# Where the second half's last scores and the meta tokens' lists are kept and sent, in a two-layer conv/attention/expert trunk on one core

## The chip, the cores and the metric

The kernel runs on one core of one Trainium2 chip. The time is device microseconds of one execution; three runs of the kernel before lie between 1829.51 and 1835.26, with the median at 1833.64.

## What is computed

272 tokens (16 meta tokens in front of 256) of 1024 float32 numbers go through two layers. Each layer is a mixer (convolution and attention, gated) and a PEER stage, in which every token picks, for each of 8 heads, 16 of 16384 experts:

```python
def _peer(h, wq, keys, u_table, v_table):
    q = (hf @ wq).reshape(T, PEER_HEADS, 2, PEER_HALF)
    s = jnp.einsum('thpd,hpnd->thpn', q, keys)
    sv, si = lax.top_k(s, PEER_TOPK)
    cand = (sv[:, :, 0, :, None] + sv[:, :, 1, None, :]).reshape(T, PEER_HEADS, PEER_TOPK * PEER_TOPK)
    cidx = (si[:, :, 0, :, None] * N_KEYS + si[:, :, 1, None, :]).reshape(...)
    top_s, top_pos = lax.top_k(cand, PEER_TOPK)
    eidx = jnp.take_along_axis(cidx, top_pos, axis=-1)
    gw = jax.nn.softmax(top_s.astype(jnp.float32), axis=-1).astype(h.dtype)
...
    def block(args):
        xb, ib, wb = args
        a = jnp.einsum('ted,td->te', u_table[ib], xb)
        act = jax.nn.gelu(a) * wb
        return jnp.einsum('te,ted->td', act, v_table[ib])
```

The output is the 256 tokens behind the meta tokens.

## The kernel before

Everything is float32, with channels on partitions. The order on each engine is the order in which the program is written; loops hand control to generators (`early`, `routes`, `gathers`, `wbuild`) a step at a time, so that work of different parts is mixed by hand. A tile's memory comes from pools; an instruction that writes a new tile waits for the last readers of what lay there.

**The end of the mixer.** `scores(i, qT_)` runs for 16 key tiles `i` (8 heads, 2 lists each). TensorE puts the scores of the first 128 tokens (`k` = 0) and of the second 128 (`k` = 1) side by side into a PSUM tile `sc`, and in layer 0 those of the meta tokens into `scm`. `top16` on VectorE picks 16 values and their places for each row: five instructions a tile, into `sv`, `si` (and `svm`, `sim` for the meta tokens). For the last four tiles (`i` of 12 and up) ScalarE first copies both halves to a tile `cp` in the mixer's pool `mp`; the second half's rows are put on the list `behind`. They are taken up only after `heads(0, 0)` and `heads(0, 1)`, which turn the first half's lists into experts (`ef`) and weights, packed into `ew` (L920). Then the mixer's pools close (`mixs.close()`).

**The expert stage** opens pools where the mixer's memory was: `X`, and `ga` with `iww` (experts and weights spread by head), `xs`, `xr`, and four buffers `gb`. Two ways lead through it. The last 160 of the 272 tokens use all experts: TensorE multiplies `xh` with every tile of `u` (the matmuls of `A`, 128 steps, each 8 matmuls that stand as 16 instructions in the trace) and later the result with every tile of `v` (the matmuls of `po`). The other tokens, two groups of 64 and 32 and in layer 0 the 16 meta tokens, gather their experts: one indirect DMA on POOL's queue brings 128 rows of `u` and `v`, 1 MB (`gb`, L1105); VectorE multiplies (L1133) and adds up (L1115, L1117). The `u` and `v` tiles come through SP's queue, four tiles of 1 MB ahead (`wraw`).

**What stands at the seam, in order.** POOL: `spread(0)`, which sends `ew` to `iww`; four gathers; `spread(1)`; then, in layer 0, eight small transfers that put the meta tokens' lists `svm`, `sim` in the layout of the others (`mv`, `mi`, L1003); then a gather for each group of rows that VectorE has added. VectorE: the four rows of `behind`; the tiles `zs`; the packing of weights (L1013 to L1015); in layer 0 `second(mv, mi, ...)`, the meta tokens' experts; then the gathers' work, mixed with `heads(1, 0)` and `heads(1, 1)` for the second half. ScalarE: `xs` (L963); two tables `tx` of the meta tokens (L806); copies of `A` to `X`; `xr` (L972). TensorE: 9 steps of `A`; the transposes of `xs` (L971); 6 steps; the transposes of `ef` for the first half (L1026); 16 steps; transposes for the next group; 5 steps; the transposes for the second half. The transposes share two PSUM buffers `wp`, so those of L1026 need a buffer that `xr` has emptied.

`idxT` (128 x 3 x 256 half-precision) and `wlo` (128 x 256 float32) are tiles that stay for the whole kernel. They are written behind the transposes of L1026 (L1027, L1028) and read by `wbuild`.

Of the kernel before, what the change touches and what calls it, by code (L numbers as in the profile page):

```python
# [7 lines left out]
F32 = mybir.dt.float32  # L8
# [3 lines left out]
U32 = mybir.dt.uint32  # L12
AF = mybir.ActivationFunctionType
# [7 lines left out]
T = 272  # L21
# [22 lines left out]
def trunk_kernel(ctx: ExitStack, tc: tile.TileContext, a: dict, out: bass.AP, dbg=None, stop=None):  # L44
    nc = tc.nc
    V, S, G, PE = nc.vector, nc.scalar, nc.gpsimd, nc.tensor
# [4 lines left out]
    def mm(o, l, r, start, stop):  # L51
        PE.matmul(o, l, r, start=start, stop=stop, skip_group_check=True)  # L52
# [81 lines left out]
    idxT = pp.tile([128, 3, 256], F16, name="idxT")  # L134
    wlo = pp.tile([128, 256], F32, name="wlo")
# [5 lines left out]
    def run_all(g):  # L141
        for _ in g:
            pass
# [32 lines left out]
    for l in range(NL):  # L176
        last = l == NL - 1
# [7 lines left out]
        rpool = rp.enter_context(tc.tile_pool(name=f"route{l}", bufs=1, side="right"))  # L185
# [40 lines left out]
        else:  # L226

            p = zp.tile([128, 512], F32, name="z", bufs=3)
# [59 lines left out]
        def attention():  # L288
# [99 lines left out]
            pk = aps()  # L388
            for i, (q0, n) in enumerate(QT):
                PE.transpose(pk[0:8, q0:q0 + n], rr[:n, i * 16 + 8:i * 16 + 16], ident[:n, :n])  # L390
            rk = mp.tile([8, T], F32, name="rk")
            S.activation(rk, pk[0:8, :T], AF.Copy)
            yield
            yield
# [364 lines left out]
        def scores(i, qT_):  # L759
            p = sp.tile([128, 512], F32, name="sc", bufs=2)  # L760
            for k, (q0, n) in enumerate(QT[:2]):
                mm(p[:, k * 128:(k + 1) * 128], qT_[:, q0:q0 + n], keys[:, i], True, True)
            if not last:

                if i % 4 == 0:
                    ohp["m"] = sp.tile([128, 512], F32, name="scm")
                q = i % 4
                mm(ohp["m"][32 * q:32 * q + 32, 0:128], qT_[:, 0:32], keys[:, i], True, True)
            if i >= 12:
                p_, p = p, mp.tile([128, T], F32, name="cp", bufs=4)[:, 0:256]  # L770
                S.activation(p, p_[:, 0:256], AF.Copy)
                if not last and i == 15:
                    m_, ohp["m"] = ohp["m"], mp.tile([128, T], F32, name="sk", bufs=2)[:, 0:128]
                    S.activation(ohp["m"], m_[:, 0:128], AF.Copy)
            rows = []
            for k in range(2):
                w = mp.tile([128, 128], F32, name=f"tkw{k}")
                rows.append((sv[:, k, i], si[:, k, i], p[:, k * 128:(k + 1) * 128], w))
            if not last and i % 4 == 3:
                rows.append((svm[:, i // 4], sim[:, i // 4], ohp["m"][:, 0:128], mp.tile([128, 128], F32, name="tkw2")))  # L780
            if i >= 12:
                behind.append(rows.pop(1))
            top16(rows)
# [100 lines left out]
        for i in range(16):  # L884
            z = ztile(t0)
            qT_ = mp.tile([128, T], F32, name="qr", bufs=2)
            S.activation(qT_[:, t0:], z, AF.Copy)
            if i == 0:
                st = sp.tile([128, 512], F32, name="st")
                sums(st[:, :TQ], sq[:, :, t0:], 1)  # L890
            if pend is not None:
                scores(i - 1, pend)
            pend = qT_
            if i == 1:
                rs = rstd(st[:, :TQ], D, TQ, "m")
            if i == 4 and not last:
                rsm = mp.tile([128, 128], F32, name="rsm")
                V.tensor_copy(rsm.rearrange("p (t h) -> p t h", h=8), rs[:, 0:16, None].to_broadcast([128, 16, 8]))
            if i == 8:

                pr_ = sp.tile([128, 512], F32, name="st")
                rsT = rpool.tile([128, 3], F32, name="rsT")
                nr = 2 if last else 3
                for k, (q0, n) in enumerate(QT[:2]):
                    PE.transpose(pr_[:, k * 128:(k + 1) * 128], rs[:, q0 - t0:q0 - t0 + n], ident)
                if not last:
                    PE.transpose(pr_[:, 256:384], rsm, ident)
            if i == 9:
                V.tensor_copy(rsT[:, 0:nr], pr_[:, 0:nr * 128].rearrange("p (k x) -> p k x", x=128)[:, :, 0])
            if i >= 9:  # L910
                next(early, None)
            if 4 <= i < 12:
                c = i - 4
                G.tensor_tensor(xh[:, c, t0:], xg[:, c, t0:], rs, op=OP.mult)  # L914
        scores(15, pend)
        run_all(early)
        run_all(heads(0, 1))

# [72 lines left out]
        def routes():  # L991
            done["e"] = ohp["ew"]
            spread(0)
            done["g"] = 1
            yield
            if not last:

                mv = rpool.tile([128, 1, 2, 16], F32, name="mv")
                mi = rpool.tile([128, 1, 2, 16], U32, name="mi")
                for q in range(4):  # L1000
                    for d_, s_ in ((mv, svm), (mi, sim)):
                        d4 = d_.rearrange("(n x) o s b -> x n o s b", x=2)[q // 2, :, 0, q % 2]
                        G.dma_start(d4, s_[32 * q:32 * q + 16])  # L1003
            r2 = ohp["r"]
            for k in range(2):
                if k:
                    yield from heads(k, 0)
                    yield from heads(k, 1)
                ew, ef = ohp["ew"], ohp["ef"]
                ts = ew[:, :, 1]  # L1010

                wh_ = r2.tile([128, 128], F16, name="w16")
                V.tensor_scalar(h8(wh_), ts, WS, None, op0=OP.mult)  # L1013
                V.tensor_copy(ef[:, 2], wh_)
                V.scalar_tensor_tensor(h8(ef[:, 3]), ts, WS, h8(ef[:, 2]), op0=OP.mult, op1=OP.subtract)  # L1015
                if k == 0:
                    if not last:
                        yield
                        im = r2.tile([128, 2, 16], F32, name="im")
                        yield from second(mv, mi, 1, rsT[:, 2:3], im, iww[-1][:, :, 1])  # L1020
                        V.scalar_tensor_tensor(iww[-1].bitcast(I32)[:, 0, 0], im[:, 0], 128.0, im[:, 1], op0=OP.mult, op1=OP.add)
                for _ in range(LAG + (7 if last and k == 0 else 0)):
                    yield
                p = pW.tile([128, 512], F32, name="wp", bufs=2)
                for q in range(4):
                    PE.transpose(p[:, q * 128:(q + 1) * 128], ef[:, q], ident)  # L1026
                S.activation(idxT[:, :, k * 128:(k + 1) * 128], p[:, 0:384].rearrange("p (a b) -> p a b", a=3), AF.Copy)  # L1027
                S.activation(wlo[:, k * 128:(k + 1) * 128], p[:, 384:512], AF.Copy)  # L1028
                yield
# [308 lines left out]
```

## Time and profile before

| | before |
|---|---|
| median of 3 runs | 1833.64 us |
| profiled execution, its own time | 1828.79 us |
| its span | 1827.0 us |
| TensorE busy | 1764.6 us (97%) |
| VectorE busy | 1143.9 us (63%) |
| ScalarE busy | 421.6 us (23%) |
| POOL busy | 324.2 us (18%) |
| DMA | 559.37 MB, mean 306 GB/s |

TensorE is busy for nearly the whole span, so what counts are the places where it is not. The slices of the span show two where its share falls inside the kernel: one around 320 to 365 us, the end of layer 0's mixer, and a lesser one around 1235 to 1280 us, the end of layer 1's. The two matrix products of the expert stage follow them, and with them the DMA queues run full.

### The profile page before, as it was taken

To read this page: it belongs to the slowest core of one execution; us is meant where nothing else is said; L and a number is where in the kernel's file an instruction comes from. 1 tells how busy PE (TensorE), PEld (TensorE's weight loads), DVE (VectorE), ACT (ScalarE), POOL (GpSimd) and SP (SyncE) were. 2 spreads that over 40 slices of the span, in tenths; PEclk is the share of its full clock that TensorE was granted. 3 is DMA by queue.
4 is the path that set the end of the run, shared out by engine and by line. 5 is a ranking of instruction groups with operands and counts; after the bars stand their busy time and mean duration, and the time that the engine had idled before them with its cause. 6 is when DMAs were issued, how large, how long until landed. Compare 5 with 4: busy or idle time off the path is not lost.

```text
span 1827.0 us, 29396 instructions
## 1 busy us (share of the span) xinstructions
PE 1764.6 (97%) x11611; PEld 1629.9 (89%) x11611; DVE 1143.9 (63%) x3101; ACT 421.6 (23%) x1225; POOL 324.2 (18%) x393
## 2 busy tenths in 40 slices
PE   9999999599999999999999999998999999999998
PEld 7678878599999989988996778898999999999998
DVE  5586269498888755445525775586978886444441
ACT  3443102234444200000014331122244431000000
POOL 0131010222211222222300220101121122222210
PEclk9999999799999999999999999999999999999999
DMA  6123434599999999999972233447999999999993
GB/s 226 70 93 116 161 117 155 193 413 393 424 424 424 424 425 421 425 422 421 417 284 85 92 116 139 162 150 312 413 425 423 423 424 420 419 413 411 413 412 147
DMA packets 80682, 559.37 MB, mean 306 GB/s; under 512 B 9176, under 2 KB 12120, under 8 KB 13080
## 3 DMA queue, kind: packets, MB, share of 16 engines
q1 hardware_dynamic: 49488, 338.54, 45.9%
q0 software_dynamic: 30336, 218.35, 28.9%
q8 instruction: 91, 1.49, 0.3%
q10 hardware_dynamic: 720, 0.60, 0.1%
q14 instruction: 47, 0.39, 0.1%
HBM read 556.18 MB, written 1.05 MB: 305 GB/s over the span
## 4 chain that ended last, share of the span: by engine, by line
PE 71%; DMA 14%; issue 10%; DVE 4%; POOL 1%; ACT 0%; SPq 0%; POOLq 0%; DVEq 0%; ACTq 0%
PE po L52 22%; PE A L52 21%; PE z L52 19%; DMA wraw<-vn 10%; PE aps L52 5%; DMA gb<-uv,iww 3%; PE wp L52 2%; DMA wraw<-u 1%; DVE va L1117 1%; DVE gb L1133 1%; PE xp L52 0%; POOL xh L914 0%; DVE ex L861 0%; DMA wraw<-w_in 0%; DVE ex L858 0%
## 5 line engine op out<-in xcount | busy, mean ns | idle before, releaser
L52 PE MATMUL A<-xh,wraw 128*128 128x160 f32 x4096 | 584.1, 302 | 3.6 <-DMA wraw<-u 2.3
L52 PE MATMUL po<-X,wraw 128*128 128x160 f32 x4096 | 569.8, 300 | 15.0 <-DMA wraw<-vn 11.5
L52 PEld LDWEIGHTS po<-X,wraw 128*128 128x128 f32 x4096 | 557.8, 190 | 25.5 <-DMA wraw<-vn 20.4
L52 PEld LDWEIGHTS A<-xh,wraw 128*128 128x128 f32 x4096 | 566.6, 192 | 5.6 <-DMA wraw<-u 3.2
L1133 DVE SCALAR_TENSOR_TENSOR gb<-gb,xr 128x1024 f32<-128x1024 f32 x208 | 254.6, 1224 | 348.0 <-DMA gb<-uv,iww 347.9
L52 PE MATMUL z<-xg,wraw 128*128 128x272 f32 (+1 forms) x1408 | 334.5, 392 | 1.4 <-DMA wraw<-w_in 0.8
L1105 POOL DMA_INDIRECT gb<-uv,iww x208 | 220.4, 1060 | 567.5 <-DVE va L1117 396.0
L52 PEld LDWEIGHTS z<-xg,wraw 128*128 128x128 f32 x1408 | 263.5, 191 | 58.1 <-issue 7.3
L1117 DVE SCALAR_TENSOR_TENSOR va<-gb,am,va 128x1024 f32<-128x1024 f32 x203 | 261.0, 1286 | 7.2
L1143 ACT ACTIVATE am<-am 128x1 f32<-128x1 f32 x208 | 41.4, 199 | 593.8 <-DVE gb L1133 593.6
L1047 ACT ACTIVATE ohA<-ohE,wlo 128x128 f16<-128x128 f16 x320 | 105.4, 427 | 10.7 <-DVE ohE L1044 7.1
L577 POOL TENSOR_TENSOR acc<-acc,cp 128x272 f32<-128x272 f32 (+1 forms) x60 | 51.1, 852 | 274.4 <-ACT cp L576 272.1
L569 DVE SCALAR_TENSOR_TENSOR acc<-upad,cols,acc 128x272 f32<-128x272 f32 (+1 forms) x180 | 83.8, 523 | 0.2
L1104 POOL COPY warm<-wraw 1x1 f32<-1x1 f32 x91 | 33.9, 372 | 264.2 <-DMA wraw<-vn 264.1
L1057 ACT ACTIVATE X<-wp 128x356 f32<-128x356 f32 (+24 forms) x80 | 26.9, 336 | 170.7 <-DVE X L1054 170.7
L1044 DVE TENSOR_TENSOR ohE<-ioh,idxT 128x512 f16<-128x512 f16 x160 | 60.4, 419 | 0.0
L52 PE MATMUL z<-xh,wraw 128*128 128x272 f32 (+1 forms) x256 | 57.3, 386 | 0.0
L52 PEld LDWEIGHTS z<-xh,wraw 128*128 128x128 f32 x256 | 48.6, 190 | 8.3
L52 PE MATMUL wp<-ohE,ohA 128*128 128x128 f16 x640 | 50.3, 219 | 0.2 <-issue 0.2
L52 PEld LDWEIGHTS <-ohA 128*128 128x128 f16 x640 | 43.4, 97 | 3.8 <-issue 0.4
L914 POOL TENSOR_TENSOR xh<-xg,rq_ym 128x272 f32<-128x272 f32 (+1 forms) x16 | 11.3, 751 | 181.8 <-DVE sv L749 93.5
L167 ACT ACTIVATE xg<-hT,cols 128x272 f32<-128x272 f32 (+1 forms) x32 | 15.5, 513 | 114.2 <-DVE hT L724 81.7
(287 smaller groups left out, 1274.0 us busy)
## 6 DMA issues: line engine op xcount, KB each, us to landing
wraw<-u SPq DMA_DIRECT2D x128, 1024.0 KB, 11.3
wraw<-vn SPq DMA_DIRECT2D x128, 1024.0 KB, 11.0
wraw<-w_in SPq DMA_DIRECT2D x27, 1024.0 KB, 4.8
wraw<-wq SPq DMA_DIRECT2D x16, 1024.0 KB, 4.8
wraw<-w_out SPq DMA_DIRECT2D x8, 1024.0 KB, 4.7
wraw<-w_mla SPq DMA_DIRECT2D x4, 1024.0 KB, 4.6
wraw<-w_conv SPq DMA_DIRECT2D x4, 1024.0 KB, 4.9
gb<-uv,iww POOLq DMA_INDIRECT x208, 11.8
```

Source lines behind the costliest of these rows:

```text
L52: PE.matmul(o, l, r, start=start, stop=stop, skip_group_check=True)
L167: S.activation(xg[:, c, c0:], hT[:, c, c0:], AF.Copy, scale=cols[l][:, base + c:base + c + 1])
L569: V.scalar_tensor_tensor(acc[:, c, t0:], u_, weight(c, k), acc[:, c, t0:], op0=OP.mult, op1=OP.add)
L577: G.tensor_tensor(acc[:, 0, t0:], acc[:, 0, t0:], u_[:, t0:], op=OP.add)
L1044: V.tensor_tensor(E[q], ioh[:, None].to_broadcast(full), pairs(q, b), op=OP.is_equal)
L1047: S.activation(A_[1][:, t // 2, :, t % 2], E[0][:, t // 2, :, t % 2], AF.Copy, scale=wlo[:, 4 * b + t:4 * b + t + 1])
L1057: S.activation(X[:, J:, s_], p[:, :, J:].rearrange("p t j -> p j t"), AF.Copy, scale=1.0 / WS)
L1104: G.tensor_copy(warm[0:1], state["w"][0:1, 0:1])
L1105: G.indirect_dma_start(out=g_, out_offset=None, in_=a[f"uv{l}"], in_offset=bass.IndirectOffsetOnAxis(ap=iww[i].bitcast(I32)[:, m // 16, 0, ...
L1117: V.scalar_tensor_tensor(vac[i], r, m_, vac[i], op0=OP.mult, op1=OP.add)
L1133: V.scalar_tensor_tensor(u_, u_, 1.0, xrs[i], op0=OP.mult, op1=OP.mult, accum_out=m_)
L1143: S.activation(m_, m_, AF.Gelu_apprx_tanh)
```

## The change

- The second half's scores of the last four tiles are copied apart from the first half's, each 128 x 128: those of tiles 12 and 13 into `wlo`, those of 14 and 15 into two thirds of `idxT`, seen as float32. The scratch that `top16` needs for them is the last third of `idxT`. The first half's stay in `cp`.
- The eight transfers to `mv` and `mi` are issued right after `scores(15)`, in front of `heads(0, 1)` and so of `spread(0)`. Their tiles are made while the mixer's pool is still open.
- Two of the mixer's tiles are dropped, their content put in others: `rk` in `mq`, `rsm` in `sk`.

```diff
-            rk = mp.tile([8, T], F32, name="rk")
+            rk = mp.tile([16, T], F32, name="mq")[0:8]
...
+            ps = [p[:, 0:128], p[:, 128:256]]
             if i >= 12:
-                p_, p = p, mp.tile([128, T], F32, name="cp", bufs=4)[:, 0:256]
-                S.activation(p, p_[:, 0:256], AF.Copy)
+                p_, ps[0] = ps[0], mp.tile([128, T], F32, name="cp", bufs=4)[:, 0:128]
+                S.activation(ps[0], p_, AF.Copy)
                 if not last and i == 15:
                     m_, ohp["m"] = ohp["m"], mp.tile([128, T], F32, name="sk", bufs=2)[:, 0:128]
                     S.activation(ohp["m"], m_[:, 0:128], AF.Copy)
+            if i >= 12:
+
+                p_, ps[1] = ps[1], wlo[:, (i - 12) * 128:(i - 11) * 128] if i < 14 else idxT.bitcast(F32)[:, i - 14]
+                S.activation(ps[1], p_, AF.Copy)
             rows = []
             for k in range(2):
-                w = mp.tile([128, 128], F32, name=f"tkw{k}")
-                rows.append((sv[:, k, i], si[:, k, i], p[:, k * 128:(k + 1) * 128], w))
+                w = idxT.bitcast(F32)[:, 2] if k and i >= 12 else mp.tile([128, 128], F32, name=f"tkw{k}")
+                rows.append((sv[:, k, i], si[:, k, i], ps[k], w))
...
-                rsm = mp.tile([128, 128], F32, name="rsm")
+                rsm = mp.tile([128, T], F32, name="sk", bufs=2)[:, 0:128]
...
         scores(15, pend)
+        if not last:
+
+            mv = rpool.tile([128, 1, 2, 16], F32, name="mv")
+            mi = rpool.tile([128, 1, 2, 16], U32, name="mi")
+            for q in range(4):
+                for d_, s_ in ((mv, svm), (mi, sim)):
+                    d4 = d_.rearrange("(n x) o s b -> x n o s b", x=2)[q // 2, :, 0, q % 2]
+                    G.dma_start(d4, s_[32 * q:32 * q + 16])
         run_all(early)
         run_all(heads(0, 1))
...
-            if not last:
-
-                mv = rpool.tile([128, 1, 2, 16], F32, name="mv")
-                mi = rpool.tile([128, 1, 2, 16], U32, name="mi")
-                for q in range(4):
-                    for d_, s_ in ((mv, svm), (mi, sim)):
-                        d4 = d_.rearrange("(n x) o s b -> x n o s b", x=2)[q // 2, :, 0, q % 2]
-                        G.dma_start(d4, s_[32 * q:32 * q + 16])
```

POOL at the seam of layer 0, before, with the semaphores that each waits for (`DMASW` are those of POOL's own transfers, eight of them, taken in turn):

```order
L989 DMA iww_2200<-ew 128x1x128 [waits DMAHW1_49,DMAHW2_49,DMAHW0_49,DMAHW4_49,DVE_49,DMAHW7_49,Activation_49,Pool_49]
L1105 DMA gb<-uv,iww_2200 128x2048 [waits DMASW0_49]
L1105 DMA gb<-uv,iww_2200 128x2048 x3
L989 DMA iww_2201<-ew 128x1x64
L1003 DMA mv<-svm 64x1x16
L1003 DMA mi<-sim 64x1x16
L1003 DMA mv<-svm 64x1x16
L1003 DMA mi<-sim 64x1x16 [waits DMASW1_49]
L1003 DMA mv<-svm 64x1x16 [waits DMASW2_49]
L1003 DMA mi<-sim 64x1x16 [waits DMASW3_49]
L1003 DMA mv<-svm 64x1x16 [waits DMASW4_49]
L1003 DMA mi<-sim 64x1x16 [waits DMASW5_49]
```

And now:

```order
L928 DMA mv<-svm 64x1x16 [waits DVE_49]
L928 DMA mi<-sim 64x1x16 [waits DVE_49]
L928 DMA mv<-svm 64x1x16
L928 DMA mi<-sim 64x1x16
L928 DMA mv<-svm 64x1x16
L928 DMA mi<-sim 64x1x16
L928 DMA mv<-svm 64x1x16
L928 DMA mi<-sim 64x1x16
L1002 DMA iww_2210<-ew 128x1x128 [waits DMAHW1_49,DMAHW0_49,DMAHW2_49,DMASW0_49,DMAHW4_49,DVE_49,DMAHW7_49,Activation_49,Pool_49]
L1110 DMA gb<-uv,iww_2210 128x2048 [waits DMASW1_49,DMASW0_49]
L1110 DMA gb<-uv,iww_2210 128x2048 [waits DMASW2_49]
```

The eight small transfers moved from behind the gathers to the front; before, the last five of them waited for the semaphores of the gathers (`DMASW1` to `DMASW4`) and of `spread(1)`, and now the gathers wait for those of the small transfers.

ScalarE at the same seam, before: the score copies of the last three tiles, the two tables and the exponential of `heads(0, 1)`, and `xs`.

```order
L771 ACTIVATE cp<-sc 128x256 [waits PE_49,Pool_49]
L887 ACTIVATE qr<-z 128x272 [waits PE_49,Activation_49]
L771 ACTIVATE cp<-sc 128x256 [waits PE_49,Pool_49] x2
L774 ACTIVATE sk<-scm 128x128 [waits PE_49]
L806 ACTIVATE tx_2089<-it_2085 128x1024 [waits DVE_49]
L806 ACTIVATE tx_2091<-it_2086 128x1024 [waits DVE_49]
L828 ACTIVATE ew<-ce,rsT 128x4x16 [waits DVE_49]
L963 ACTIVATE xs<-xh 128x1024 [waits DMAHW1_49,DMAHW2_49,DMAHW0_49,DMAHW4_49,DVE_49,DMAHW7_49,Activation_49,Pool_49]
```

And now:

```order
L772 ACTIVATE cp<-sc 128x128 [waits PE_49,Pool_49]
L779 ACTIVATE wlo<-sc 128x128
L892 ACTIVATE qr<-z 128x272 [waits PE_49,Activation_49]
L772 ACTIVATE cp<-sc 128x128 [waits PE_49,Pool_49]
L779 ACTIVATE idxT<-sc 128x128
L772 ACTIVATE cp<-sc 128x128 [waits PE_49,Pool_49]
L775 ACTIVATE sk<-scm 128x128 [waits PE_49]
L779 ACTIVATE idxT<-sc 128x128
L811 ACTIVATE tx_2099<-it_2095 128x1024 [waits DVE_49]
L811 ACTIVATE tx_2101<-it_2096 128x1024 [waits DVE_49]
L833 ACTIVATE ew<-ce,rsT 128x4x16 [waits DVE_49]
L976 ACTIVATE xs<-xh 128x1024 [waits DMAHW2_49,DMAHW1_49,DMAHW4_49,DMAHW0_49,DMAHW7_49,Activation_49,Pool_49]
```

Each copy of 128 x 256 became two of 128 x 128, the second into `wlo` or `idxT`, and among the semaphores that `xs` waits for VectorE's (`DVE`) is gone.

## Rows read from the trace of the kernel before

**Rows 1.** TensorE's waits, whole span: line, releaser, us in total, times, longest.

```profile
PE wp L1026 <- ACT xr L972: 15.2, 2, 14.9
PE po L52 <- DMA wraw<-vn: 11.5, 35, 0.8
```

**Rows 2.** Timeline of TensorE, seam of layer 0: start, us, instruction, count, idle before.

```profile
302.81 19.80 PE L52 MATMUL A<-xh,wraw 128*128 128x160 f32 x144 [0.41 <-issue]
327.43 1.97 PE L971 MATMUL wp<-ident,xs 128*128 128x128 f32 x8 [4.81 <-ACT xs L963]
329.19 15.27 PE L52 MATMUL A<-xh,wraw 128*128 128x160 f32 x96
359.34 1.11 PE L1026 MATMUL wp<-ident,ef 128*128 128x128 f32 x4 [14.87 <-ACT xr L972]
360.24 36.84 PE L52 MATMUL A<-xh,wraw 128*128 128x160 f32 x256
...
415.37 0.80 PE L1026 MATMUL wp<-ident,ef 128*128 128x128 f32 x2 [2.46 <-DVE ef L1014]
```

**Rows 3.** Timeline of VectorE, the same seam.

```profile
306.33 0.29 DVE L757 FIND_INDEX8 sim<-svm,tkw 128x8 uint32<-128x128 f32 x1
...
320.08 0.29 DVE L920 SCALAR_TENSOR_TENSOR ew<-ef 128x128 int32<-128x128 f32 x1
...
325.87 0.29 DVE L757 FIND_INDEX8 si<-sv,tkw 128x8 uint32<-128x128 f32 x1
...
327.44 0.29 DVE L1015 SCALAR_TENSOR_TENSOR ef<-ew,ef 128x128 f32<-128x128 f32 x1
352.31 0.17 DVE L801 CAST it<-mi 128x16 f16<-128x16 uint32 x1 [24.57 <-DMA mi<-sim]
...
360.72 1.22 DVE L1133 SCALAR_TENSOR_TENSOR gb<-gb,xr 128x1024 f32<-128x1024 f32 x1
...
372.56 1.23 DVE L1133 SCALAR_TENSOR_TENSOR gb<-gb,xr 128x1024 f32<-128x1024 f32 x1 [1.03 <-DMA gb<-uv,iww]
...
415.35 0.29 DVE L1015 SCALAR_TENSOR_TENSOR ef<-ew,ef 128x128 f32<-128x128 f32 x1
```

**Rows 4.** Timeline of ScalarE, the same seam.

```profile
302.44 0.27 ACT L774 ACTIVATE sk<-scm 128x128 f32<-128x128 f32 x1
...
326.32 1.06 ACT L963 ACTIVATE xs<-xh 128x1024 f32<-128x1024 f32 x1 [15.00 <-DVE si L757]
...
358.69 1.08 ACT L972 ACTIVATE xr<-wp 128x512 f32<-128x512 f32 x2
```

**Rows 5.** Timeline of POOL, the same seam.

```profile
326.87 0.79 POOL L989 DMA_DIRECT2D iww<-ew  x1 [77.24 <-issue]
...
343.74 0.50 POOL L1003 DMA_DIRECT2D mi<-sim  x1 [4.48 <-DMA gb<-uv,iww]
...
349.68 0.50 POOL L1003 DMA_DIRECT2D mi<-sim  x1 [0.16 <-issue]
364.31 1.74 POOL L1105 DMA_INDIRECT gb<-uv,iww  x1 [14.14 <-DVE va L1115]
```

**Rows 6.** Timelines at the seam of layer 1: VectorE, POOL, TensorE, VectorE again.

```profile
1239.30 0.29 DVE L920 SCALAR_TENSOR_TENSOR ew<-ef 128x128 int32<-128x128 f32 x1
...
1246.03 0.65 POOL L989 DMA_DIRECT2D iww<-ew  x1 [67.57 <-issue]
...
1246.64 1.97 PE L971 MATMUL wp<-ident,xs 128*128 128x128 f32 x8 [5.57 <-ACT xs L963]
...
1273.96 1.23 DVE L1133 SCALAR_TENSOR_TENSOR gb<-gb,xr 128x1024 f32<-128x1024 f32 x1 [1.04 <-DMA gb<-uv,iww]
```

**Rows 7.** Stretches: length, busy of PE, PEld, DVE, ACT, POOL, PEclk, DMA, GB/s.

```profile
323.00:416.00 93.00, 67.95 (x457) 66.85 (x458) 63.46 (x259) 26.03 (x45) 20.83 (x24) 0.85 0.77 312
370.00:409.00 39.00, 38.83 (x288) 38.59 (x286) 35.93 (x140) 11.32 (x21) 6.73 (x6) 1.00 1.01 423
1247.00:1257.00 10.00, 10.00 (x60) 10.00 (x59) 1.24 (x2) 3.88 (x8) 4.44 (x5) 0.77 0.70 237
```

## The prediction

> **What bounds the kernel now.** The first view to read is the list of waits of TensorE over the whole span. Its longest single wait is one of 14.9 us: the transposes of L1026 waiting for the copies `xr` of ScalarE; 35 small waits for `vn` tiles make another 11.5 us [rows 1]. The rest of the span TensorE works, so a change is worth what it takes out of such gaps, as long as nothing else is late at the same place.
>
> The second view is the timeline of TensorE at the seam between mixer and expert stage of layer 0 [rows 2]. The reader is to see three holes. After the first 144 matmuls of `A` it is idle for 4.81 us, until the copy `xs` is there. After the next 96 it is idle for 14.87 us. After 256 and 80 more it stands at the transposes of the second half, whose last pair starts at 415.37. Then nothing is late until the `vn` tiles. The matmuls of `A` run at 19.80/144 = 0.1375 us where the clock is full, and 96 of them took 15.27 us, not 13.2, after the first hole; over 323 to 416 the granted clock is 0.85 on average, between the two levels of 1.2 and 2.4 GHz [rows 2, 7].
>
> The third view, the other engines, says why. Hole one: VectorE finishes `ew` at 320.4 but then takes the four left-over score rows of the second half, to 326.16; `xs` starts on ScalarE at 326.32 and POOL's `iww` at 326.87 [rows 3 to 5]. Both write memory that those rows still hold. Hole two: VectorE is free at 327.73 and stands until 352.31, because the meta tokens' `mi` is not there [rows 3]. POOL issues these eight transfers behind four gathers, and the later ones of them wait for gathers to land (4.48 us in one of them); the last is issued at 349.68 [rows 5]. ScalarE's `xr` stands behind the meta tokens' work and ends at 359.77 [rows 4].
>
> **The change, part by part: layer 0.** *The small transfers.* Eight issues of some 0.50 us [rows 5] now stand in front of `iww`. They wait for `svm` and `sim`, complete at 306.6 [rows 3], so POOL has issued them by 306.6 + 8 x 0.5 = 310.6. The last one in the trace was used 352.31 - 349.68 = 2.6 us after its issue, so they land by 313.3, where POOL had nothing to do before 320.4. Nothing is queued behind them but `iww`, and VectorE wants them only at 327.7: 14 us of cover. A price above zero appears if that cover is gone (third rival).
>
> *The kept scores.* The four rows are read where nothing of the next stage is placed, so `xs` can run long before TensorE asks, at 322.6, and the hole of 4.81 us closes. `iww` waits for `ew` alone: 320.37 + 0.7 (the lag that 326.16 to 326.87 shows) = 321.1, or 5.8 us earlier [rows 3, 5]. ScalarE pays with a second copy per tile: 0.27 us [rows 4], four times a layer, of which only those of the last tile stand in front of the first `A`: 0.3 us a layer. Below zero this can't go, as the work is added.
>
> *What is late next.* VectorE starts on `mi` at 327.7, and from there `xr` takes 359.77 - 352.31 = 7.5 us: ready at 335.2 [rows 3, 4]. TensorE comes to L1026 at 322.6 + 0.9 + 13.2 = 336.7, so hole two closes, with 1.5 us to spare. It then runs 256 and 80 matmuls and eight transposes, and reaches the second half's transposes at 336.7 + 0.6 + 35.2 + 1.0 + 11.0 = 384.5 [rows 2]. VectorE isn't there yet. Three estimates of when `ef` is ready, 415.64 before [rows 3]:
> - VectorE alone. From the first L1133 at 360.72 to 415.64 are 54.9 us, 1.4 of it waiting. The first now comes at 327.7 + (360.72 - 352.31) = 336.1; without any wait the end is 389.6. That is the early bound.
> - The gathers. In layer 1, where no meta tokens stand between, the fifth gather was used 1273.96 - 1246.03 = 27.9 us after the issue of `iww` [rows 6]. Counted from 321.1 that is 349.0; VectorE alone would be there by 347.9 (372.56 - 360.72 = 11.8 after 336.1). From the fifth to `ef` it took 415.64 - 372.56 = 43.1, hence 392.1.
> - The DMA. From 323 to 416 it moved 93 us x 312 GB/s; at the 423 GB/s of a full stretch these are 68.6 us, hence 391.6 if it is full from 323. Layer 1's first ten microseconds of gathers ran at 237 GB/s, which costs 4.4 us: 396.0, the late bound [rows 7].
> I take 393.5, between the second and the third. The gain of layer 0 is 415.64 - 393.5 = 22.1, less 0.3: **21.8 us** (19.3 to 25.7). It is not the 19.7 us of the two holes plus the slow clock taken one by one: TensorE gets them all back, and then gives about 9 us to the wait at the second half, which had been some 6.
>
> *From there to the layer's end.* TensorE, VectorE and the DMA queue stand in the same relation as before at 416, so the shift stays. The `vn` waits may grow by about what the DMA lags in the third estimate; that is inside the range.
>
> **Layer 1** has no meta tokens. Hole one is 5.57 us there; `iww` goes from 1246.03 to 1239.59 + 0.7 = 1240.3, 5.7 us earlier [rows 6]. TensorE alone could gain more than the hole, since the clock doesn't fall, but VectorE's chain through the gathers moves by the 5.7, and TensorE waits for it again at the second half. Less 0.3: **5.4 us** (4 to 8).
>
> **The other edits** (`rk` in `mq`, `rsm` in `sk`) rename memory; each former user is done many instructions before. They cost nothing.
>
> **Sum.** 21.8 + 5.4 = 27.2 us. The profiled execution took 1828.79 us for a span of 1827.0, and would take 1801.6. The three runs have their median at 1833.64, 4.9 above it; the median less 27.2 is **1806.4**.
>
> **Rivals.**
> *The wait only moves on, further than I think.* The second half's transposes sit behind VectorE and it behind the gathers. If each of the gathers after the fourth came 1 us later than in layer 1, because TensorE now draws `u` tiles without a pause, then `ef` is ready seven gathers, 7 us, later: at 400.5, and the sum is 20.2 us: 1813.4. For it: TensorE gets no pause in which the DMA catches up. Against: 370 to 409 was such a stretch, with the DMA full, and gathers kept coming [rows 2, 7].
>
> *The change does only half.* If something else held the mixer's memory as long, hole one would stay and only the transfers would be early. `iww` would stay at 326.9; the gain is 16 us in layer 0 and none in layer 1: 1817.6. Against: the instruction order shows VectorE gone from the waits of `xs`.
>
> *The small transfers are issued slowly.* They now fall where VectorE is busy without a gap, and a gather's issue beside a busy VectorE took 1.74 us [rows 5]. Decisive is whether eight issues end by 320.4: they may take 1.7 us each, over three times the 0.50. At five times, 2.5 us, they end at 326.6 and `iww` is where it was: layer 0 gains 16 us and the time is 1812. The Trainium skill has a rule that speaks for this (page "SBUF — State Buffer", section "Who interferes with whom"): a DMA of the GpSimd queue needs GpSimd to write its descriptors, and certain VectorE operations, copies and casts among them, block it for their whole length. By that rule the result is this rival's only if such operations fill the stretch; between 306 and 314 most of the list are maxima, comparisons and two-input operations, so I give it little.
>
> *Slower: the weights come last.* With gathers from 323 on, the DMA is full for the whole `A` stage. A `u` tile feeds 32 matmuls, 4.4 us; about 58 tiles are still to come in layer 0 at 323. If each came 0.47 us behind TensorE's need, the 27 us are spent; at 0.6 us the kernel is 8 us slower, 1841. For it: the 35 waits for `vn` show that full DMA can make weights late. Against: from 370 to 409 TensorE was busy for 38.83 of 39 us under a full DMA, with no more gathers outstanding now than then [rows 1, 7].
>
> **How the numbers follow.** Forecast 0.80; the wait moved on 0.08; half 0.02; slow issues 0.04; slower 0.04; and 0.02 that two of the weaker cases meet and leave no change. A measurement here tells about 0.3%, 5.5 us, from no change. All but the last two are faster: 0.94, same 0.02, slower 0.04. The range: the early bound in both layers gives 25.7 + 8 = 33.7, 1800, and I allow 2 us more for where the median of a few runs falls; the other end takes in the moved wait and the slow issues, 1815.
>
> **What would show it.** In the changed trace: transposes of `xs` follow the 144 matmuls without a hole, in both layers; the eight small transfers lie between 306 and 313 and `iww` near 321; no hole at the first half's transposes, though only by 1.5 us; a wait of some 9 us at the second half's, ended by VectorE; the clock full through 323 to 380. Wrong if `iww` is issued after 326, if the second half's `ef` comes after 400, or if waits for `u` tiles appear between 340 and 600.

## The result, and the profile after

The changed kernel takes 1812.76 us (median of 4 runs, 1810.55 to 1814.4) where the kernel before takes 1833.95 beside it (1829.51 to 1835.26): a ratio of 0.989, interval 0.987 to 0.991. It is 1.1% faster, 21 us. The time lies in the range, 6.4 us above the forecast. The profiled execution took 1810.55 us for a span of 1808.8; before, 1828.79 for 1827.0. So of the 27.2 us that the sum gave for the profiled executions 18.2 came.

TensorE at the seam of layer 0, timeline of the changed kernel (columns as in [rows 2]; L984, L1031 and L1138 are L971, L1026 and L1133 of before):

```profile
303.08 19.80 PE L52 MATMUL A<-xh,wraw 128*128 128x160 f32 x144 [0.58 <-ACT idxT L779]
322.72 1.04 PE L984 MATMUL wp<-ident,xs 128*128 128x128 f32 x8
323.59 13.21 PE L52 MATMUL A<-xh,wraw 128*128 128x160 f32 x96
336.63 0.60 PE L1031 MATMUL wp<-ident,ef 128*128 128x128 f32 x4
...
390.13 0.47 PE L1031 MATMUL wp<-ident,ef 128*128 128x128 f32 x1 [4.82 <-ACT xr L985]
393.43 0.48 PE L1031 MATMUL wp<-ident,ef 128*128 128x128 f32 x1 [2.83 <-DVE ef L867]
396.37 0.80 PE L1031 MATMUL wp<-ident,ef 128*128 128x128 f32 x2 [2.46 <-DVE ef L1019]
396.96 9.18 PE L52 MATMUL A<-xh,wraw 128*128 128x160 f32 x48
```

Holes one and two of [rows 2] are gone: the transposes of `xs` follow the 144 matmuls, those of the first half the next 96, and the 96 now run at full speed. What is left are three waits at the second half's transposes, 10.1 us together, and matmuls that start at the lower clock behind them: 48 of them take 9.18 us, where behind the shorter wait of before they took 8.04. Before:

```profile
415.97 8.04 PE L52 MATMUL A<-xh,wraw 128*128 128x160 f32 x48
```

The first of the three waits is put down to ScalarE's `xr`, but this too stands behind VectorE: ScalarE does it at 389.50, right after the `am` that waits for the gather's product of 388.13. The stretches show the clock of that (columns as in [rows 7]):

```profile
330.00:390.00 60.00, 54.28 (x399) 53.56 (x397) 50.19 (x202) 21.54 (x39) 10.08 (x10) 0.99 1.01 423
390.00:402.00 12.00, 6.58 (x23) 5.85 (x24) 11.65 (x24) 2.64 (x9) 3.77 (x4) 0.50 0.70 261
```

From 330 to 390 the DMA is full and the clock at its upper level; from 390 to 402 it is granted 0.50, the lower level, after TensorE has stood for ten microseconds with pieces of work between.

POOL, same seam. The eight small transfers now stand in front, and `iww` is issued at 321.10, but its first gather waits for it (fourth column: the wait and what ended it):

```profile
306.49 0.71 POOL L928 DMA_DIRECT2D mv<-svm  x1 [56.80 <-DVE si L757]
...
310.16 0.61 POOL L928 DMA_DIRECT2D mi<-sim  x1
...
321.10 0.57 POOL L1002 DMA_DIRECT2D iww<-ew  x1 [10.33 <-issue]
326.12 1.03 POOL L1110 DMA_INDIRECT gb<-uv,iww  x1 [4.46 <-DMA iww<-ew]
```

VectorE, same seam: the first five gathers' products, and the last `ef` of the second half.

```profile
335.57 1.22 DVE L1138 SCALAR_TENSOR_TENSOR gb<-gb,xr 128x1024 f32<-128x1024 f32 x1
337.23 1.23 DVE L1138 SCALAR_TENSOR_TENSOR gb<-gb,xr 128x1024 f32<-128x1024 f32 x1 [0.35 <-DMA gb<-uv,iww]
342.36 1.23 DVE L1138 SCALAR_TENSOR_TENSOR gb<-gb,xr 128x1024 f32<-128x1024 f32 x1 [3.03 <-DMA gb<-uv,iww]
347.30 1.23 DVE L1138 SCALAR_TENSOR_TENSOR gb<-gb,xr 128x1024 f32<-128x1024 f32 x1 [1.52 <-DMA gb<-uv,iww]
352.74 1.23 DVE L1138 SCALAR_TENSOR_TENSOR gb<-gb,xr 128x1024 f32<-128x1024 f32 x1 [1.18 <-DMA gb<-uv,iww]
...
396.35 0.29 DVE L1020 SCALAR_TENSOR_TENSOR ef<-ew,ef 128x128 f32<-128x128 f32 x1
```

The gathers land some 5 us apart, and VectorE waits for four of these five. In layer 1 (POOL, TensorE, and VectorE's fifth product) hole one of [rows 6] is gone as well, and the same wait is there at the second half:

```profile
1222.81 0.64 POOL L1002 DMA_DIRECT2D iww<-ew  x1 [61.79 <-issue]
1226.78 1.00 POOL L1110 DMA_INDIRECT gb<-uv,iww  x1 [3.33 <-DMA iww<-ew]
```

```profile
1203.93 19.80 PE L52 MATMUL A<-xh,wraw 128*128 128x160 f32 x144 [0.64 <-ACT idxT L779]
...
1290.80 0.45 PE L1031 MATMUL wp<-ident,ef 128*128 128x128 f32 x1 [4.02 <-DVE am L1117]
1294.73 0.48 PE L1031 MATMUL wp<-ident,ef 128*128 128x128 f32 x1 [3.48 <-DVE ef L867]
1296.27 0.80 PE L1031 MATMUL wp<-ident,ef 128*128 128x128 f32 x2 [1.07 <-DVE ef L1019]
1296.86 10.27 PE L52 MATMUL A<-xh,wraw 128*128 128x160 f32 x64
```

```profile
1254.86 1.23 DVE L1138 SCALAR_TENSOR_TENSOR gb<-gb,xr 128x1024 f32<-128x1024 f32 x1 [1.60 <-DMA gb<-uv,iww]
```

TensorE at the same places before:

```profile
1221.28 19.80 PE L52 MATMUL A<-xh,wraw 128*128 128x160 f32 x144 [0.58 <-issue]
...
1315.39 0.65 PE L1026 MATMUL wp<-ident,ef 128*128 128x128 f32 x2 [1.22 <-DVE ef L1014]
1315.88 8.86 PE L52 MATMUL A<-xh,wraw 128*128 128x160 f32 x64
```

Counted from the first `A`, `iww` is issued 5.9 us earlier than before (18.88 us against 24.75), yet the last transposes come only 1.8 us earlier (92.34 against 94.11).

### The profile page after: what moved, and what is told of

It reads as the page before. It is cut to its first block, busy times and chain, and to the rows that moved or that the text cites. A ratio compares the mean times of both kernels' runs of the same rounds, so it can differ in the third digit from the quotient of the medians.

```text
span 1808.8 us, 29412 instructions
## 1 busy us (share of the span) xinstructions
PE 1760.8 (97%) x11611; PEld 1626.7 (90%) x11611; DVE 1144.0 (63%) x3101; ACT 423.1 (23%) x1233; POOL 336.4 (19%) x393
## 4 chain that ended last, share of the span: by engine, by line
PE 73%; DMA 15%; issue 6%; DVE 5%; ACT 0%; POOL 0%; SPq 0%; POOLq 0%; DVEq 0%; ACTq 0%
PE po L52 22%; PE A L52 21%; PE z L52 21%; DMA wraw<-vn 10%; PE aps L52 5%; DMA gb<-uv,iww 3%; PE wp L52 2%; DMA wraw<-u 1%; DVE va L1122 1%; DVE gb L1138 1%; DMA iww<-ew 0%; DVE ex L866 0%; PE xp L52 0%; PE sc L52 0%; DMA wraw<-w_in 0%
## 5 line engine op out<-in xcount | busy, mean ns | idle before, releaser
L1138 DVE SCALAR_TENSOR_TENSOR gb<-gb,xr 128x1024 f32<-128x1024 f32 x208 | 254.5, 1223 | 348.0 <-DMA gb<-uv,iww 347.6
L1148 ACT ACTIVATE am<-am 128x1 f32<-128x1 f32 x208 | 41.4, 199 | 598.2 <-DVE gb L1138 598.1
L1109 POOL COPY warm<-wraw 1x1 f32<-1x1 f32 x91 | 49.6, 545 | 286.0 <-DMA wraw<-vn 286.0
L1059 DVE SCALAR_TENSOR_TENSOR X<-wp,X 128x156 f32<-128x156 f32 (+24 forms) x80 | 38.3, 479 | 6.9 <-PE wp L52 6.6
```

Of the source, the lines that this page charges most:

```text
L1059: V.scalar_tensor_tensor(X[:, :J, s_], p[:, :, :J].rearrange("p t j -> p j t"), 1.0 / WS, X[:, :J, s_], op0=OP.mult, op1=OP.mult)
L1109: G.tensor_copy(warm[0:1], state["w"][0:1, 0:1])
L1138: V.scalar_tensor_tensor(u_, u_, 1.0, xrs[i], op0=OP.mult, op1=OP.mult, accum_out=m_)
L1148: S.activation(m_, m_, AF.Gelu_apprx_tanh)
```

## The experiments

Three theories were to be told apart. **A**: a TensorE that does not pause draws `u` tiles without a pause, `iww` and the first gathers share the DMA with them and come later, and the chain of gathers sets the second half's transposes. **C**: each hole of TensorE counts by itself. **B**: POOL's transfers are late because VectorE is busy beside POOL. Some expectations name variants of A (A2, A3) and rivals of those (A4, D); each says there what it stands for.

**One part alone: the transfers, without the kept scores** (`e1_transfers_only`).

```diff
-            ps = [p[:, 0:128], p[:, 128:256]]
...
-                p_, ps[0] = ps[0], mp.tile([128, T], F32, name="cp", bufs=4)[:, 0:128]
-                S.activation(ps[0], p_, AF.Copy)
+                p_, p = p, mp.tile([128, T], F32, name="cp", bufs=4)[:, 0:256]
+                S.activation(p, p_[:, 0:256], AF.Copy)
...
```

> The change with the eight small transfers in front alone; the second half's rows stay in the mixer's memory. Theory A (after the change the wait at the second half's transposes, set by the gathers, is what ends last, so hole one by itself is worth little): iww at 326.9 as before, but it lands within 2 us; hole one is back (4.8 us in layer 0, 5.6 in layer 1), hole two is gone, and the second half's transposes end at 399 to 401; layer 1 as before. Time 2 to 6 us above the full change. Theory C (each hole of TensorE counts by itself): hole one and its slow clock cost 7 us in layer 0 and 8 in layer 1, so about 15 us above the full change.

Measured: 1814.75 us, ratio 0.991 (0.989 to 0.993). Holes one are back, 4.80 us in layer 0 and 5.55 in layer 1, and `iww` is issued 7 us later, at 328.19, though it lands after 1.90 us. All that is some 2 us slower than the whole change, less than the runs of either kernel scatter. This kernel is what the prediction's rival "the change does only half" describes: the rival gave 16 us of gain, and 17.6 were measured. The last transposes:

```profile
400.77 0.80 PE L1026 MATMUL wp<-ident,ef 128*128 128x128 f32 x2 [2.46 <-DVE ef L1014]
```

C falls: two holes, 10.4 us together, cost 2, where C gave 15. A holds: `iww` starts 7.1 us later than in the changed kernel, but from it to the product of the fifth gather pass 29.6 us instead of 31.6, and the last transposes come only 4.4 us later, of which 1.1 stand already at the first `A` (304.21).

**The other part alone: kept scores, the transfers behind the gathers again** (`e2_scores_only`; the loop of `mv` and `mi` moved back to `routes`).

> The change with the kept scores alone; the eight transfers stay behind the gathers. All theories: hole one gone, iww near 321, hole two still there, since mi comes behind the gathers: used at 345 to 350, first half's transposes at 352 to 358 (359.3 before). Theory A: 3 to 6 us less than the kernel before from layer 0 and 1 to 2 from layer 1, about 1828. Theory C: the 4.8 us and 5.6 us of hole one plus slow clock come off in full, about 1820.

Measured: 1826.71 us, ratio 0.998 (0.997 to 0.999). Hole two grows, as TensorE comes there sooner:

```profile
356.12 1.12 PE L1031 MATMUL wp<-ident,ef 128*128 128x128 f32 x4 [19.64 <-ACT xr L977]
```

So the transfers carry the gain; the kept scores bring 5.6 us alone and 2 on top. That fits A, which forecast about 1828, and not C, with about 1820.

**Hole one put back into the change** (`e7_hole_back`). `xs` again waits until VectorE has done the four rows; `iww` does not:

```diff
+            if i == 0:
+                V.memset(xs[0:1, 0:1], 0.0)
```

> The full change, but xs of the first group waits for the second half's four rows again (one element of it is written behind them), so hole one is back in both layers while iww and the small transfers stay early. Theory A: TensorE gives 4 to 5 us to hole one and gets them back at the second half's transposes, where it waits 11 us (layer 0) and 8.6 (layer 1) anyway; time within 3 us of the full change, either way. Theory C: 5 us and the slow clock in each layer, 12 to 15 us above the full change.

Measured: 1807.38 us, ratio 0.987 (0.986 to 0.989). The hole costs nothing: by the medians the kernel is 5 us faster than the change, more than theory A's 3, though the intervals overlap. Four of its five runs lie below all nine runs of the change (those of `e12_change_again` among them), and the fifth lies among them. It is also faster than `e1_transfers_only`, run beside it, which has the same hole but a late `iww`. TensorE and VectorE in layer 0:

```profile
328.32 1.97 PE L986 MATMUL wp<-ident,xs 128*128 128x128 f32 x8 [5.22 <-ACT xs L978]
...
392.38 0.66 PE L1033 MATMUL wp<-ident,ef 128*128 128x128 f32 x2 [0.17 <-DVE ef L1021]
```

```profile
339.28 1.22 DVE L1140 SCALAR_TENSOR_TENSOR gb<-gb,xr 128x1024 f32<-128x1024 f32 x1
343.45 1.23 DVE L1140 SCALAR_TENSOR_TENSOR gb<-gb,xr 128x1024 f32<-128x1024 f32 x1 [0.77 <-DMA gb<-uv,iww]
349.74 1.23 DVE L1140 SCALAR_TENSOR_TENSOR gb<-gb,xr 128x1024 f32<-128x1024 f32 x1 [1.97 <-DMA gb<-uv,iww]
```

TensorE stands 5.22 us early on and comes to the second half's transposes when they are ready; they are 4 us earlier than in the change. (A wait of 2.27 us for one-hot tiles follows at 401.82.) `iww` lands no faster (4.39 us), but the third to fifth products are 3.0 to 3.9 us earlier. The stretch in which the first gathers travel says why, first of the change, then of this kernel:

```profile
326.00:336.00 10.00, 10.00 (x76) 10.00 (x75) 9.04 (x55) 7.46 (x11) 4.51 (x5) 1.00 0.87 349
```

```profile
326.00:336.00 10.00, 7.68 (x39) 7.69 (x40) 9.01 (x57) 8.40 (x12) 4.52 (x5) 0.66 0.76 272
```

TensorE did half as many matmuls (39 records against 76) and the core moved 272 GB/s instead of 349. From 322 to 334 SP issues two `u` tiles in the change (325.96 and 331.84) and none here: the `u` tiles that TensorE did not ask for left room.

**Less on the DMA** (`e3_half_u`). Ten `u` tiles of each layer, from the one asked for at the seam on, are loaded by half, and their first half is used twice; so it leaves out work:

```diff
...
-                nc.sync.dma_start(r, srcs[k])
+                h = 1 if half(k) else 2
+                nc.sync.dma_start(r[:, 0:h], srcs[k][:, 0:h])
...
```

> The full change, but for ten u tiles of each layer (those fetched while the gathers begin) half of the bytes are left out; the second half of each such tile is computed with the first. Theory A (the u tiles that an unpausing TensorE draws make iww and the first gathers late): iww lands within 2.5 us of its issue (4.5 in layer 0 and 3.3 in layer 1 with the full change), the first gather of layer 1 is used within 6 us of its issue (8.6), and the second half's transposes end 4 to 8 us earlier in both layers. Theory B (POOL's transfers are late because GpSimd writes their descriptors beside a busy VectorE): iww lands as late as with the full change, and so do the transposes within 2 us.

Measured: one run, 1797.73 us. The gathers' start in layer 0:

```profile
322.35 0.58 POOL L1006 DMA_DIRECT2D iww<-ew  x1 [10.32 <-issue]
325.53 1.03 POOL L1114 DMA_INDIRECT gb<-uv,iww  x1 [2.60 <-DMA iww<-ew]
```

`iww` lands after 2.60 us instead of 4.46 and in layer 1 after 1.79 instead of 3.33; the last transposes come 86.3 us after the first `A` instead of 93.3, and in layer 1 after 85.4 instead of 92.3. So with nothing taken away but load on the DMA they come 7 us earlier in each layer.

**The same with nothing left out: one `u` tile held back** (`e9_hold_tile`). POOL copies an element of `iww` into the buffer of one `u` tile of each layer before SP may load it. POOL does so behind its first four gathers, so in layer 0 SP issues this tile at 328.73 instead of 320.74, and the next one, issued at 325.96 in the change, right behind it:

```diff
+                if k in (30 + 7, 188 + 7):
+                    G.tensor_copy(r[0:1, 0, 0:1], state["iww"][0:1, 0, 0, 0:1])
...
```

> The full change, but one u tile a layer (the one asked for at 320.7, just ahead of iww at 321.1), and those behind it on SP's queue, are held back until POOL has iww and has issued the four gathers, some 7 us. Theory A (u tiles in flight delay iww and the first gathers): iww lands within 2.5 us (4.5 and 3.3), the second half's transposes end 1.5 to 4 us earlier in each layer, and time is 2 to 6 us below the full change, unless TensorE then waits for the held tiles. Theory B (descriptors beside a busy VectorE): iww lands as late as before; no gain.

Measured: 1805.07 us (1802.04 to 1810.49), ratio 0.986 (0.984 to 0.988); all four runs lie below the nine of the change. POOL, TensorE, and the stretches in which `iww` travels, first of this kernel, then of the change:

```profile
320.95 0.58 POOL L1004 DMA_DIRECT2D iww<-ew  x1 [10.32 <-issue]
323.11 1.03 POOL L1113 DMA_INDIRECT gb<-uv,iww  x1 [1.59 <-DMA iww<-ew]
```

```profile
338.64 4.61 PE L52 MATMUL A<-xh,wraw 128*128 128x160 f32 x16 [4.19 <-DMA wraw<-u]
...
392.58 0.66 PE L1034 MATMUL wp<-ident,ef 128*128 128x128 f32 x2 [1.33 <-DVE ef L1022]
```

```profile
321.00:323.00 2.00, 2.00 (x18) 2.00 (x17) 1.90 (x12) 0.00 (x0) 0.52 (x1) 1.00 0.14 33
321.00:326.00 5.00, 5.00 (x40) 5.00 (x40) 4.76 (x30) 0.00 (x0) 0.57 (x1) 1.00 0.67 223
```

VectorE is busy for 1.90 of the first 2 us, in the change as here, and yet `iww` lands after 1.59 us: B falls, A holds. TensorE pays 4.19 us for the late tile (5.84 in layer 1) and gets more back.

**The first `iww` on ScalarE's queue** (`e4_iww_act`).

```diff
-            G.dma_start(iww[g], done["e"][q0 - META:q0 - META + n])
+            (S if g == 0 else G).dma_start(iww[g], done["e"][q0 - META:q0 - META + n])
```

> The full change, but the first iww transfer of each layer is issued on ScalarE's queue in place of POOL's. Theory A: the same DMA engines carry it beside the u tiles, so it lands no sooner (3 us or more after its issue) and time is that of the full change within 3 us. Theory B: it lands within 2 us, the first gathers start 2 us earlier in both layers, and time is 2 to 5 us below the full change.

Measured: 1812.57 us, ratio 0.989 (0.988 to 0.991). ScalarE's queue and POOL:

```profile
319.73 0.60 ACTq L1002 DMA_DIRECT2D iww<-ew  x1
```

```profile
325.84 1.03 POOL L1110 DMA_INDIRECT gb<-uv,iww  x1 [15.94 <-DMA iww<-ew]
```

Issued 1.4 us sooner, it releases the first gather 0.3 us sooner, and 0.9 us of both stand already at the first `A` (302.19 against 303.08). Who issues is not what delays it. The Trainium skill (page "DMA: Bandwidth & Descriptors", section "Issuing engines are not separate DMA queues") says that transfers of different engines run on the same DMA engines and interleave; this run agrees, with 5.5 us from the end of the issue to the gather on ScalarE's queue and 4.46 on POOL's.

**The four rows taken later** (`e6_rows_late`; the four calls on `behind` moved into the steps of `A`, in layer 0 behind the first gather's product, in layer 1 behind the packing of weights).

> The full change, but VectorE takes up the second half's four rows later: in layer 0 behind the meta tokens' experts, in layer 1 between the first gathers. So in layer 1 VectorE is nearly idle while iww is under way. Theory A: iww of layer 1 still lands 3 us or more after its issue. Theory B: within 2 us. For the time: the 5.9 us of rows move into VectorE's waits for gathers (7.3 us in layer 0, 14.8 in layer 1), so if VectorE's chain to the second half's ef is what ends last, it ends 2 to 5 us earlier in layer 1; if the gathers alone set it, nothing moves.

Measured: 1811.98 us, ratio 0.989 (0.987 to 0.990). The last transposes are at 396.99, and `iww` lands after 4.61 and 3.51 us. On B it says nothing, since VectorE was filled all the same: in layer 0 with other work (4.52 of the 5 us from 321 to 326), and in layer 1, where the expectation had it nearly idle, with the rows themselves, which it took up at 1223.10 (4.76 of the 5 us from 1222 to 1227). It shows that the rows' place in layer 0 is worth nothing: VectorE waits for gathers anyway.

**TensorE asked to come later to the transposes** (`e5_lag`; five steps of `A` more in front of the second half's, where the expectation speaks of seven, and the rate of the weights' building raised to catch up).

> The full change, but TensorE comes to the second half's transposes seven steps of A (15 us) later, and the one-hot products behind them are spread a little denser, so that the wait of 11 us (layer 0) and 8.6 us (layer 1) has other work in its place. Theory A2 (from 331 on the DMA is full and sets the pace, so a wait of TensorE that is filled comes back as waits for u and vn tiles): the wait is gone, but time falls by no more than 4 us a layer, 1805 to 1812. Theory D (the wait is TensorE's own loss): 9 to 12 us a layer with the slow clock behind it, 1789 to 1795.

Measured: 1813.1 us, ratio 0.989 (0.988 to 0.991). No wait is left at the transposes, but the next thing that stands behind VectorE's queue has one:

```profile
420.96 1.01 PE L52 MATMUL wp<-ohE,ohA 128*128 128x128 f16 x8 [16.89 <-issue]
```

The one-hot tiles which this product takes are built by VectorE behind products of gathers, four of them some 5 us apart (400.59 to 416.08):

```profile
416.08 1.23 DVE L1138 SCALAR_TENSOR_TENSOR gb<-gb,xr 128x1024 f32<-128x1024 f32 x1 [2.30 <-DMA gb<-uv,iww]
...
419.76 0.76 DVE L1049 TENSOR_TENSOR ohE<-ioh,idxT 128x512 f16<-128x512 f16 x2
```

The wait moved (in layer 1 it is 12.19 us), and the time is that of the change. So D falls. A2's time is missed by 1 us, and its reason is not borne out: no wait for `u` tiles is left, and those for `vn` stay at 11.4 us. The label "issue" hides the releaser here; the rows of VectorE tell it.

**Fewer gathers in front** (`e10_rate`): VectorE takes fewer gathers per step of `A` up to step 40 and more behind it.

```diff
-RU = (1.45, 1.35)
+RE = (1.15, 1.1)
+RU = (1.5, 1.43)
...
-                some_gathers(RU[l])
+                some_gathers(RE[l] if j < 40 else RU[l])
```

> The full change, but up to step 40 of A VectorE takes up gathers at 1.15 (layer 1: 1.1) parts a step in place of 1.45 (1.35), and at 1.5 (1.43) after it; nothing is left out. Theory A3 (VectorE's rows for the second half stand in its queue behind gathers that land 5 us apart beside the u tiles; fewer gathers ahead of them, and they come sooner): some three gathers fewer stand ahead, the second half's transposes end 6 to 12 us earlier in each layer (396.4 in layer 0), the waits there fall below 5 us, and the time is 1798 to 1806. Rival A4 (the DMA's bytes set the end of each layer, whatever the order): the wait goes, and comes back as waits for u and vn tiles; 1809 to 1813.

Measured: 1804.67 us (1803.21 to 1806.51), ratio 0.985 (0.984 to 0.987), faster than both kernels and with nothing left out. The last transposes of layer 0:

```profile
386.42 0.80 PE L1032 MATMUL wp<-ident,ef 128*128 128x128 f32 x2 [1.07 <-DVE ef L1020]
```

Nine products of gathers stand in front of them, eleven in the change, and they are ready 10 us earlier (in layer 1 some 6, counted from the first `A`). A4 falls with the time, but what it said is there in part, for some of the gain is given back: layer 1 begins only 3.7 us earlier (1200.20 against 1203.93), and the waits for `vn` tiles in both layers grow from 11.0 us in 35 to

```profile
PE po L53 <- DMA wraw<-vn: 15.0, 43, 1.1
```

and the gathers left over are done beside the `v` tiles. By the profiled executions the whole gain over the change is 5.4 us, by the medians beside it 7.7.

**Both at once** (`e11_hold_rate`), and **the change again beside them** (`e12_change_again`).

> The held u tile and the lower first rate together. Theory A3: the second half's transposes don't wait at all, but the held tile still costs TensorE 4 to 6 us a layer, so about as fast as the better of the two alone, 1798 to 1806. Rival A4: as the held tile alone, 1803 to 1808, since the bytes are the same.

> The full change once more, on the same chip and beside the two that follow: 1810 to 1814.

Measured: 1806.11 us (1805.35 to 1811.5), ratio 0.987 (0.985 to 0.989); the change 1812.39, ratio 0.990 (0.989 to 0.991). The two edits do not add up: both shorten the same wait. (The time stands at the upper end of A3's range and within A4's, so this run doesn't tell those two apart.) The change again shows how far its chain repeats: its fifth product came 33.1 us after the issue of `iww`, 31.6 in the first trace. With both edits no wait is left at the second half's transposes, and the held tile still costs its 4.02 and 6.14 us.

## Why the prediction was right, and where it was not

**Right by its steps.** The small transfers were issued from 306.49 to 310.77 (306.6 to 310.6 in the text), `iww` at 321.10 (321.1). `xr` was ready at 334.84 (335.2), so hole two closed with 1.8 us to spare at 336.63 (336.7). The second copies took 0.27 us and the first `A` began 0.27 us later. TensorE came to the second half's transposes at 385.3 (384.5), with the clock full until there, and waited 10.1 us (9) for the chain of gathers. The waits of `A` for `u` tiles stayed at some 2 us (2.1 against 2.3) and those for `vn` at 11, so the slower rival did not come. (Waits for `u` tiles between 340 and 600, a sign of being wrong by the prediction's own words, are there, 0.72 and 0.30 us in front of the second half's transposes, but too small to count.) Nor did slow issues: the eight took 0.55 to 0.71 us each beside a busy VectorE. The rule weighed with that rival (the Trainium skill, page "SBUF — State Buffer", section "Who interferes with whom") is seen at work in no run here: with one tile held, `iww` landed after 1.59 us while VectorE was busy for 95% of the stretch. As its operations there were maxima and comparisons, this is no test of copies and casts.

**Wrong: the way from `iww` to the fifth gather.** The prediction took 27.9 us from layer 1 of before. Measured:

| | `iww` issued | landed after | to the fifth product | from there to the last transposes |
|---|---|---|---|---|
| before, whence the two terms came | 1246.03 | 1.59 | 27.9 (layer 1) | 42.8 (layer 0) |
| changed, layer 0 | 321.10 | 4.46 | 31.6 | 43.6 |
| changed, layer 1 | 1222.81 | 3.33 | 32.1 | 41.4 |
| changed, run again, layer 0 | 320.72 | 4.37 | 33.1 | 43.1 |
| hole put back, layer 0 | 321.33 | 4.39 | 28.4 | 42.6 |
| one tile held, layer 0 | 320.95 | 1.59 | 29.0 | 42.7 |
| `u` tiles halved, layer 0 | 322.35 | 2.60 | 26.0 | 42.3 |

The second step of that chain was right within a microsecond; the first was 3.7 us short. It came from a stretch in which TensorE had stood for 5.57 us in hole one just before `iww` went out [rows 6]. The `u` buffers were full then: SP issued one at 1238.93 and the next at 1252.34. So `iww` landed in 1.59 us, and until 1252.34 the first gathers shared the DMA with no new `u` tile. The stretch in which `iww` and the first gathers go out, before:

```profile
1246.00:1250.00 4.00, 3.36 (x14) 3.37 (x15) 0.69 (x4) 3.97 (x7) 2.08 (x3) 0.50 0.11 27
```

The change takes that hole away, and so the condition under which the 27.9 had been measured. Half `u` tiles, a held tile and a hole put back each bring it back to 26 to 29 in layer 0 and 25 to 30 in layer 1: that is shown. In layer 0 the last `ef` was there at 396.35 + 0.29 = 396.6 where 393.5 was forecast, 0.6 past the late bound of 396.0; the prediction had that size in its third estimate and then went between the second and the third. The rival "the wait only moves on" had the right reason, a TensorE that draws `u` tiles without a pause, but not the place: it laid 7 us on the gathers after the fourth, while 3.7 us were lost on the way to the fifth and under 1 behind it. That its 1813.4 is nearer to the measured time than the forecast is luck, since it counted no loss in layer 1.

**Wrong: layer 1.** The term was 5.4 us, on the argument that the chain of gathers moves by as much as `iww`. `iww` moved by 5.9, the fifth product by 1.8 (50.93 us after the first `A`, 52.68 before), the last transposes by 1.8, and the 64 matmuls behind a longer wait took 10.27 us instead of 8.86. What was left is 0.9 (18.2 in all less the 17.35 by which layer 1 began earlier). The same cause as in layer 0, but here nearly the whole term.

**Mis-sized: what follows the wait.** The prediction let the shift of 416 stand unchanged to the layer's end. TensorE resumed 19.0 us earlier (415.97 to 396.96), and layer 1 began 17.35 earlier. Of the 1.65 us lost, 1.1 lie in the 48 matmuls at the lower clock, 9.18 us where they took 8.04 after the shorter wait of before; the rest was not placed.

**The sum.** Against 27.2: 2.8 us too much at the second half's transposes, 1.7 behind them, 4.5 in layer 1, together 9.0. The median missed by only 6.4, because the median of the kernel before lies about 5 us above its profiled execution, as the text had it, and that of the changed kernel only 2.2. That part of the agreement is luck.

**What stays open.** That TensorE's early hole is free follows from the runs; that putting it back is a gain of 5 us does not, since the intervals overlap and the spans differ by 3.2 us.

## What to carry to other kernels

A duration read from a stretch holds with what the other engines did in it: before it is used, ask whether the change takes that away, here the pause in which the weights' queue stood still. When a hole of an engine closes, look at the next place where that engine waits, and count in the gain only as far as the chain that ends there moves. Where such a chain is paced by transfers, it is shortened by what stands in it, as two gathers fewer in front brought the end of the wait 10 and 6 us forward in the two layers and 5 to 8 us in the whole, while another queue, a later transpose or another place for compute work were worth nothing.

## What the runs showed of the hardware

The same transfer of 64 KB on POOL's queue landed after 1.6 us with the weights' queue idle (33 GB/s in that stretch) and after 4.4 to 4.5 us beside it, where the core moved 223 GB/s with the DMA engines busy for 0.67 of the time, far from the 423 of a full stretch; from ScalarE's queue it was no faster. So a small transfer on which a long chain hangs is slow well before the DMA is full. And a TensorE that idled 5.22 us, and then ran at a granted clock of 0.66 on average from 326 to 336, cost nothing here, where it would else have waited as long further on.
